# A two-layer decoder trunk in split float32: two loads of each weight tile in place of three

## The chip, the cores and the metric

The kernel runs on one core of a Trainium2 chip. The metric is device time in microseconds of one execution. Three runs of the kernel before gave 2343.18, 2343.87 and 2344.66 us; the median is 2343.87.

## The reference

Two layers run over 264 tokens, 256 of a prompt and 8 samples, which share the weights (the samples come with states of their own). Everything is float32. Per layer:

```
n = rmsnorm(x);  z = n @ W_in                      # 2048 x 5136, columns split among four groups
  A short gated conv   B GLA (gated linear attention)   C long causal conv   D spatial gating
x = x + concat(A, B, C, D) @ W_o                   # 2048 x 2048
x = x + (silu(m @ W_gate) * (m @ W_up)) @ W_down   # m = rmsnorm(x); 2048 x 5632, 5632 x 2048
```

A final rmsnorm follows, and the new states are returned as well.

## The kernel before

**Layout.** Activations lie feature-major: xs is [128 features, 16 tiles, 264 tokens]. A weight matrix is stationary, 128x128 at a time, and the 264 tokens are the moving columns, so that one matmul makes 128 output features of all tokens in PSUM.

**Split products.** TensorE runs on fp32r operands, which keep fewer bits than float32. So each operand is split into a high part (a rounded copy, made by ScalarE) and a low part (the rest, made by VectorE): weights into wh and wl (lines 285 and 286), activations into xh and xl, hh and hl, or the y tiles (split_x, emit_y, ev_ab, ev_u). A product is the sum of three: wh with the high activations (L300), wh with the low ones (L301), wl with the high ones (L302). For each of them the 128x128 weight tile is loaded anew, so wh is loaded twice and wl once.

**stream.** All large products go through stream (line 265): 512 output columns of a matrix, four column tiles m of 128, over all its row tiles of 128. It works in chunks of KC = 2 row tiles: SyncE's queue loads 512 KB into raw (four buffers), ScalarE makes wh, VectorE makes wl (three buffers each), and TensorE does for each of the four column tiles and two row tiles the three matmuls. Four PSUM banks collect the sums over the whole stream; then evac(m, psum) takes each away. There are 80 streams and 752 chunks: per layer ten of the projection W_in (c2, c1, r, q with k, v, vd, u, ac, ax, ab, in this order; r has 16 columns more, in a fifth bank, lines 304 to 314), four of W_o, 22 of gate and up (pairs, 512 columns each), four of W_down.

**PSUM.** Eight banks: five in the pool ps_w, three in ps_m. In the projections, in W_o and in the first pair of gate and up, a stream's sums come from ps_w alone (the small products of the layer use ps_m); with wide=True they go round all eight by the counter turn.

**Work beside the streams.** Per projection stream VectorE and ScalarE evacuate four tiles and do what the groups need. The long convolution (cc, line 474) runs in the background on VectorE: step_back puts 1.75 of its instructions on average behind each chunk's wl.

**The order.** The kernel is written through a tile framework. It has a scheduler which orders each engine's instructions when the program is built; each engine then runs its list in order and waits by semaphores for operands and for buffers to come free. What is written next to each other need not stand so in the list.

Of the kernel before, what the change touches and what calls it, by code (L numbers as in the profile page):

```python
# [17 lines left out]
P = 128  # L18
# [12 lines left out]
KC = 2  # L31
CW = 31
COL = dict(ax=0, ab=512, ac=1024, q=1536, k=1792, v=2048, r=2560, lr=3072,
# [7 lines left out]
def hybrid_trunk_kernel(  # L41
# [13 lines left out]
    raw_p = ctx.enter_context(tc.tile_pool(name="raw", bufs=4))  # L55
    sp_p = ctx.enter_context(tc.tile_pool(name="sp", bufs=3))
# [49 lines left out]
    xs = act.tile([P, KT, T], F32, tag="xs", name="xs")  # L106
    xh = act.tile([P, KT, T], F32R, tag="xh", name="xh")
    xl = act.tile([P, KT, T], F32R, tag="xl", name="xl")
    xhs = [xh[:, k, :] for k in range(KT)]
    xls = [xl[:, k, :] for k in range(KT)]  # L110
# [37 lines left out]
    # Sample tokens: the parts of both convolutions that lie in the states, in three pieces  # L148
# [30 lines left out]
    def newton(var, y, hv, t, inv=1.0):  # L179
        """y = 1/sqrt(inv * var + eps) to full float32 precision."""  # L180
# [16 lines left out]
    def token_means(ps, c0, src, ones, start=True, stop=True):  # L197
        """ps[:, c0:c0+3] = column means of src [P, T], for tokens 0.., 128.. and the last 128."""
# [4 lines left out]
    def split_x(par, row):  # L203
        """Split of gain * x for the tensor engine."""
        for k in range(KT):
            g = par[:, k % 4, row + k // 4:row + k // 4 + 1]
            actf(xh[:, k, :], xs[:, k, :], AF.Identity, scale=g)
            stt(out=xl[:, k, :], in0=xs[:, k, :], scalar=g, in1=xh[:, k, :].bitcast(F32),
                op0=ALU.mult, op1=ALU.subtract)

    def add_squares(acc, g):
        """acc += squares of x tiles 2g, 2g+1."""
# [18 lines left out]
    def rms_x(acc):  # L231
        """1/rms of x on every partition, from the sums of squares of its tiles."""
# [9 lines left out]
    def step_back(ins):  # L242
        """Some instructions of the work in the background, behind ins on VectorE."""
# [21 lines left out]
    def stream(W, col0, ncol, kts, rh, rl, evac, wide=False):  # L265
# [6 lines left out]
        for m in range(nm):  # L272
            turn[0] = (turn[0] + 1) % 8
            if wide and turn[0] >= 5:
                pts.append(psm("pwx"))
            elif m < 4:
                pts.append(ps_w.tile([P, T], F32, tag="w", name=f"pw{m}"))
            else:
                pts.append(psm("pwx"))
        for c in range(0, len(kts), KC):  # L280
            k0 = kts[c]
            r = early.pop(0) if early else load_w(W, len(kts) * P, col0, ncol, k0)
# [7 lines left out]
            if back:  # L290
                step_back(sub)
            for m in range(nm):
                for j in range(KC):
                    kk = k0 + j
                    first = c == 0 and j == 0
                    last = c + KC >= len(kts) and j == KC - 1
                    if m < 4:
                        o = pts[m][:, :T]
                        a = wh[:, j, m * P:(m + 1) * P]
                        mm(out=o, lhsT=a, rhs=rh[kk], start=first, stop=False)  # L300
                        mm(out=o, lhsT=a, rhs=rl[kk], start=False, stop=False)  # L301
                        mm(out=o, lhsT=wl[:, j, m * P:(m + 1) * P], rhs=rh[kk],  # L302
                           start=False, stop=last)
                    else:
                        def both():
                            mm(out=pts[m][:2 * nx, :T], lhsT=wh[:, j, 512:512 + 2 * nx],
# [713 lines left out]
```

## Time and profile before

| what | value |
|---|---|
| median of the runs | 2343.87 us |
| profiled execution: span | 2341.9 us |
| TensorE, mean granted clock | 0.993 |
| DMA, mean over the span | 176 GB/s, 412.44 MB |
| TensorE waiting for VectorE's wl | 14.4 us in 9 waits |

The page of the profile gives each engine's busy time, the chain of work that ended last, and the costliest groups of instructions (line, engine, operation, output and inputs, shapes, count, busy time, mean length, idle time before and what ended it). PE is TensorE, PEld its weight loads, which run beside it, DVE is VectorE, ACT ScalarE. A timeline gives start, length and row; windows give, for a stretch, busy time and count of each engine, the granted clock (PEclk) and the share of the DMA engines. The profiled execution took the span plus what lies around it; the median stands 2.0 us above the span.

### The profile page before, as it was taken

To read this page: it belongs to the slowest core of one execution; us is meant where nothing else is said; L and a number is where in the kernel's file an instruction comes from. 1 tells how busy PE (TensorE), PEld (TensorE's weight loads), DVE (VectorE), ACT (ScalarE), POOL (GpSimd) and SP (SyncE) were. 2 spreads that over 40 slices of the span, in tenths; PEclk is the share of its full clock that TensorE was granted. 3 is DMA by queue.
4 is the path that set the end of the run, shared out by engine and by line. 5 is a ranking of instruction groups with operands and counts; after the bars stand their busy time and mean duration, and the time that the engine had idled before them with its cause. 6 is when DMAs were issued, how large, how long until landed. Compare 5 with 4: busy or idle time off the path is not lost.

```text
span 2341.9 us, 44256 instructions
## 1 busy us (share of the span) xinstructions
PE 2300.4 (98%) x18656; PEld 2275.3 (97%) x18656; DVE 1464.6 (63%) x2084; ACT 1003.0 (43%) x1248; POOL 214.0 (9%) x266
## 2 busy tenths in 40 slices
PE   9989999999999999999998999999999999999997
PEld 8889999999999999999998999999999999999997
DVE  6999966555655555444469998665555555544444
ACT  5534454444444444444344445444444444433433
POOL 3852000000000000000039110000000000000000
PEclk9999999999999999999999999999999999999999
DMA  7436555555555555555563455555555555555553
GB/s 237 139 117 183 171 185 185 180 179 183 180 188 182 181 182 181 180 179 179 180 200 124 136 182 169 186 179 182 181 180 180 189 180 181 182 181 178 174 178 128
DMA packets 208875, 412.44 MB, mean 176 GB/s; under 512 B 14001, under 2 KB 14067, under 8 KB 208644
## 3 DMA queue, kind: packets, MB, share of 16 engines
q1 hardware_dynamic: 204644, 400.53, 52.5%
q0 software_dynamic: 4032, 9.09, 1.5%
q8 instruction: 146, 2.39, 0.4%
q14 instruction: 53, 0.43, 0.1%
HBM read 404.25 MB, written 6.29 MB: 175 GB/s over the span
## 4 chain that ended last, share of the span: by engine, by line
PE 92%; DVE 5%; issue 1%; DMA 1%; ACT 0%; POOL 0%; SPq 0%; DVEq 0%; ACTq 0%
PE pw L300 22%; PE pw L301 22%; PE pw L302 22%; PE pwx L300 8%; PE pwx L301 8%; PE pwx L302 8%; DVE wl L286 1%; DVE cc L474 1%; DVE qd L593 1%; DVE bb L538 0%; DVE att L603 0%; PE ps_os L710 0%; PE ps_lv L601 0%; DMA raw<-in_w_in_dram 0%; DVE dd L586 0%
## 5 line engine op out<-in xcount | busy, mean ns | idle before, releaser
L286 DVE TENSOR_TENSOR wl<-raw,wh 128x1024 fp32r<-128x1024 f32 x752 | 932.4, 1241 | 734.2 <-ACT wh L285 733.3
L285 ACT ACTIVATE wh<-raw 128x1024 fp32r<-128x1024 f32 (+1 forms) x752 | 795.8, 1060 | 1197.7 <-PE pw L301 680.9
L302 PE MATMUL pw<-xh,wl 128*128 128x264 f32 x3136 | 887.3, 287 | 14.5 <-DVE wl L286 14.4
L300 PE MATMUL pw<-xh,wh 128*128 128x264 f32 x3136 | 894.9, 287 | 6.3 <-DVE qk L548 2.9
L301 PE MATMUL pw<-xl,wh 128*128 128x264 f32 x3136 | 893.5, 286 | 0.0
L302 PEld LDWEIGHTS pw<-xh,wl 128*128 128x128 f32 x3136 | 590.1, 190 | 18.3 <-DVE wl L286 16.6
L300 PEld LDWEIGHTS pw<-xh,wh 128*128 128x128 f32 x3136 | 593.6, 190 | 10.5 <-DVE qk L548 3.3
L301 PEld LDWEIGHTS pw<-xl,wh 128*128 128x128 f32 x3136 | 593.8, 189 | 5.6 <-issue 5.0
L300 PE MATMUL pwx<-xh,wh 128*128 128x264 f32 x960 | 273.0, 285 | 0.0
L302 PE MATMUL pwx<-xh,wl 128*128 128x264 f32 x960 | 272.4, 284 | 0.0
L301 PE MATMUL pwx<-xl,wh 128*128 128x264 f32 x960 | 272.3, 284 | 0.0
L301 PE MATMUL pw<-hl,wh 128*128 128x264 f32 x880 | 250.8, 286 | 0.0
L300 PE MATMUL pw<-hh,wh 128*128 128x264 f32 x880 | 250.4, 285 | 0.0
L302 PE MATMUL pw<-hh,wl 128*128 128x264 f32 x880 | 248.9, 285 | 0.0
L300 PEld LDWEIGHTS pwx<-xh,wh 128*128 128x128 f32 x960 | 180.9, 189 | 0.1
L302 PEld LDWEIGHTS pwx<-xh,wl 128*128 128x128 f32 x960 | 180.9, 189 | 0.0
L301 PEld LDWEIGHTS pwx<-xl,wh 128*128 128x128 f32 x960 | 180.7, 188 | 0.0
L300 PEld LDWEIGHTS pw<-hh,wh 128*128 128x128 f32 x880 | 165.9, 189 | 0.0
L301 PEld LDWEIGHTS pw<-hl,wh 128*128 128x128 f32 x880 | 165.8, 188 | 0.0
L302 PEld LDWEIGHTS pw<-hh,wl 128*128 128x128 f32 x880 | 165.2, 189 | 0.1
L301 PE MATMUL pwx<-hl,wh 128*128 128x264 f32 x528 | 150.8, 286 | 0.0
L300 PE MATMUL pwx<-hh,wh 128*128 128x264 f32 x528 | 150.2, 285 | 0.0
(303 smaller groups left out, 2413.8 us busy)
## 6 DMA issues: line engine op xcount, KB each, us to landing
raw<-in_w_gate_dram SPq DMA_DIRECT2D x176, 512.0 KB
raw<-in_w_up_dram SPq DMA_DIRECT2D x176, 512.0 KB
raw<-in_w_down_dram SPq DMA_DIRECT2D x176, 512.0 KB
raw<-in_w_in_dram SPq DMA_DIRECT2D x144, 512.0 KB
raw<-in_w_o_dram SPq DMA_DIRECT2D x64, 512.0 KB
raw<-in_w_in_dram SPq DMA_DIRECT2D x16, 528.0 KB
xp<-in_x_prompt_dram SPq DMA_DIRECT2D x4, 512.0 KB
s<-in_state_gla_dram POOLq DMA_DIRECT2D x16, 128.0 KB, 7.5
```

What stands on the lines that cost most here:

```text
L285: actf(wh[:, :, :ncol], r[:, :, :ncol], AF.Copy)
L286: sub = tt(out=wl, in0=r[:, :, :512], in1=wh[:, :, :512].bitcast(F32), op=ALU.subtract)
L300: mm(out=o, lhsT=a, rhs=rh[kk], start=first, stop=False)
L301: mm(out=o, lhsT=a, rhs=rl[kk], start=False, stop=False)
L302: mm(out=o, lhsT=wl[:, j, m * P:(m + 1) * P], rhs=rh[kk], start=False, stop=last)
L474: yield stt(out=cc[:, t, 0:NPT], in0=cext[:, t, k:k + NPT], scalar=col(t, k), in1=cc[:, t, 0:NPT], op0=ALU.mult, op1=ALU.add)
L593: tt(out=qd[half(r), q, :, r, :].rearrange("p s (n w) -> p s n w", w=h), in0=qz[half(r), q, 0:NPT].rearrange("p (s n w) -> p s n w", s=2, ...
```

## The change

High and low activations of a tile now lie side by side in one tile of 528 columns (xw, hw, yw, yaw): 264 high, then 264 low. With LB = 136 the products of a row tile become:

- wh with the first 400 columns, that is all high and the first 136 low ones, in one matmul (L324), into a bank of 400 columns: sums of the high part in 0:264, of those low ones in 264:400;
- wl with the 264 high columns (L325), as before;
- the other 128 low columns become stationary themselves: 128 tokens by 512 output columns, one matmul with wh as the moving side for all four column tiles (L313), into a bank pp of its own.

At the end of a stream ScalarE copies pp to SBUF (psb), and four matmuls with psb as the stationary side and the identity as the moving one transpose it into the columns 136:264 of the four sums (last_low, L297). The 136 low columns in 264:400 are added by VectorE: in W_o and W_down straight into xs (add_x, two additions for a tile where there was one), elsewhere after a ScalarE copy (L343, L344) into the sums in PSUM, before evac. A stream thus takes five banks where it took four. The high and low parts of the y tiles are split per smaller tile and lie in other buffers of the mixer (s0, vb, t10, qk). The arithmetic is the same sum of three products.

The diff, cut to its core:

```
+LB = 136
+    xw = act.tile([P, KT, 2 * T], F32R, tag="xw", name="xw")
+    def split_plain(w, src):
+        h, lo = (w[:, :T], w[:, T:]) if len(w.shape) == 2 else (w[:, :, :T], w[:, :, T:])
+        actf(h, src, AF.Copy)
+        tt(out=lo, in0=src, in1=h.bitcast(F32), op=ALU.subtract)
+
+    def add_x(i, ps, low):
+        tt(out=xs[:, i, :], in0=xs[:, i, :], in1=ps, op=ALU.add)
+        tt(out=xs[:, i, :LB], in0=xs[:, i, :LB], in1=low, op=ALU.add)
...
-        for m in range(nm):
+        for m in range(-1, nm):
             turn[0] = (turn[0] + 1) % 8
-            if wide and turn[0] >= 5:
+            if m == 4 or wide and turn[0] >= 5:
                 pts.append(psm("pwx"))
...
+        pp, pts = pts[0], pts[1:]
+        def last_low(m):
+            mm(out=pts[m][:, LB:T], lhsT=psb[:, m * P:(m + 1) * P], rhs=ident_r, start=False, stop=True)
...
+            for j in range(KC):
+                mm(out=pp, lhsT=xws[k0 + j][:, T + LB:], rhs=wh[:, j, :512],
+                   start=c == 0 and j == 0, stop=end and j == KC - 1)
+            if end:
+                psb = lo_p.tile([P, 512], F32R, tag="psb", name="psb")
+                actf(psb, pp, AF.Copy)
...
-                        mm(out=o, lhsT=a, rhs=rh[kk], start=first, stop=False)
-                        mm(out=o, lhsT=a, rhs=rl[kk], start=False, stop=False)
-                        mm(out=o, lhsT=wl[:, j, m * P:(m + 1) * P], rhs=rh[kk],
-                           start=False, stop=last)
+                        mm(out=pts[m][:, :T + LB], lhsT=hi, rhs=x[:, :T + LB], start=first, stop=False)
+                        mm(out=pts[m][:, :T], lhsT=lo, rhs=x[:, :T], start=False, stop=False)
...
+                if end and 1 <= m < 4:
+                    last_low(m - 1)
+            if end:
+                last_low(3)
         for m in range(nm):
+            o = pts[m][:P if m < 4 else 2 * nx]
+            low = o[:, T:T + LB]
+            if parts:
+                evac(m, o[:, :T], low)
+                continue
+            t = tmp.tile([P, LB], F32, tag="t1", name="low", bufs=6)[:P if m < 4 else 2 * nx]
+            actf(t, low, AF.Copy)
+            tt(out=o[:, :LB], in0=o[:, :LB], in1=t, op=ALU.add)
+            evac(m, o[:, :T])
```

Three places of the order follow; a name's number tells one buffer from another.

TensorE, first layer, from the end of the stream vd (sums pw..., the last chunk's wh and wl) to the first chunks of the stream u (pw0). Before:

```order
L301 MATMUL pw3_2197<-xl_94,wh_2422 128x264
L302 MATMUL pw3_2197<-xh_93,wl_2423 128x264
L300 MATMUL pw0_2517<-xh_93,wh_2523 128x264
L301 MATMUL pw0_2517<-xl_94,wh_2523 128x264
L302 MATMUL pw0_2517<-xh_93,wl_2524 128x264
```

Now, at the same place (pw-1 is the bank pp of the new stream):

```order
L325 MATMUL pw3_2059<-xw_96,wl_2243 128x264
L297 MATMUL pw0_2056<-ident_r_97,psb_2250 128x128
L297 MATMUL pw1_2057<-ident_r_97,psb_2250 128x128
L297 MATMUL pw2_2058<-ident_r_97,psb_2250 128x128
L297 MATMUL pw3_2059<-ident_r_97,psb_2250 128x128
L313 MATMUL pw-1_2349<-wh_2356,xw_96 128x512 x2
L313 MATMUL pw-1_2349<-wh_2381,xw_96 128x512 x2
L313 MATMUL pw-1_2349<-wh_2407,xw_96 128x512 x2
L324 MATMUL pw0_2350<-xw_96,wh_2356 128x400
L325 MATMUL pw0_2350<-xw_96,wl_2357 128x264
```

The four small products stand at the end of the old stream, and the low-row products of three chunks stand ahead of the new stream's first column tile.

VectorE at the same edge; dv is the evacuation of vd, os and cc are other work, wl are the splits of the new stream's chunks. Before:

```order
L286 TENSOR_TENSOR wl_2555<-raw_2552,wh_2554 128x1024
L474 SCALAR_TENSOR_TENSOR cc_915<-cext_259,par0_827,cc_915 128x256
L751 TENSOR_TENSOR dv_2192<-pw0_2194,rb_634 128x264
L751 TENSOR_TENSOR dv_2192<-pw1_2195,rb_634 128x264
L474 SCALAR_TENSOR_TENSOR cc_915<-cext_259,par0_827,cc_915 128x256
L751 TENSOR_TENSOR dv_2192<-pw2_2196,rb_634 128x264
L718 COPY_PREDICATED os_2139<-smask_90,ps_os_2094 32x128
L751 TENSOR_TENSOR dv_2192<-pw3_2197,rb_634 128x264
L718 COPY_PREDICATED os_2139<-smask_90,ps_os_2094 32x128 x2
L286 TENSOR_TENSOR wl_2587<-raw_2584,wh_2586 128x1024
```

Now:

```order
L306 TENSOR_TENSOR wl_2408<-raw_2405,wh_2407 128x1024
L502 SCALAR_TENSOR_TENSOR cc_861<-cext_263,par0_773,cc_861 128x256
L199 TENSOR_TENSOR nt_2011<-hv_2009,rs_2010 128x9
L344 TENSOR_TENSOR pw0_2056<-pw0_2056,low_2272 128x136
L344 TENSOR_TENSOR pw1_2057<-pw1_2057,low_2277 128x136
L344 TENSOR_TENSOR pw2_2058<-pw2_2058,low_2282 128x136
L344 TENSOR_TENSOR pw3_2059<-pw3_2059,low_2287 128x136
L502 SCALAR_TENSOR_TENSOR cc_861<-cext_263,par0_773,cc_861 128x256
L200 TENSOR_TENSOR nt_2011<-nt_2011,rs_2010 128x9
L779 TENSOR_TENSOR dv_2053<-pw0_2056,rb_592 128x264
```

The split of the new stream's third chunk (wl_2408) stands ahead of the evacuation of the first tile, where the third one (wl_2587) stood behind all four; the four additions stand ahead of it too.

TensorE in the feed-forward stage of the first layer, between an up stream and the next gate stream (the old sums are 6912 to 6915, the new ones 7149 to 7152), now:

```order
L313 MATMUL pw-1_7148<-wh_7179,xw_96 128x512
L297 MATMUL pw0_6912<-ident_r_97,psb_7092 128x128
L297 MATMUL pw1_6913<-ident_r_97,psb_7092 128x128
L297 MATMUL pw2_6914<-ident_r_97,psb_7092 128x128
L297 MATMUL pw3_6915<-ident_r_97,psb_7092 128x128
L324 MATMUL pwx_7151<-xw_96,wh_7155 128x400
```

Here the small products stand inside the new stream; its fourth column tile (pw3_7152) comes first 25 matmuls after them.

More of the change, by code (lines that the diff above doesn't have):

```diff
@@ L106, in hybrid_trunk_kernel @@
     xs = act.tile([P, KT, T], F32, tag="xs", name="xs")
[L107 to L110, printed above, removed]
+    xw = act.tile([P, KT, 2 * T], F32R, tag="xw", name="xw")
+    xws = [xw[:, k, :] for k in range(KT)]
+    ident_r = cst.tile([P, P], F32R, tag="ident_r", name="ident_r")
+    nc.vector.tensor_copy(ident_r, ident)
+    def split_plain(w, src):
[5 more added lines that the diff above has]
+        tt(out=xs[:, i, :LB], in0=xs[:, i, :LB], in1=low, op=ALU.add)
     def load_rows(l, dma):
@@ L263, in load_w, with stream @@
         return r
-    def stream(W, col0, ncol, kts, rh, rl, evac, wide=False):
+    def stream(W, col0, ncol, kts, xws, evac, wide=False, parts=False):
         nm = (ncol + P - 1) // P
@@ L315, in stream @@
-        for m in range(nm):
-            evac(m, pts[m][:P if m < 4 else 2 * nx, :T])
+                        hi, lo = (w[:, j, m * P:(m + 1) * P] for w in (wh, wl))
+                        mm(out=pts[m][:, :T + LB], lhsT=hi, rhs=x[:, :T + LB], start=first, stop=False)
+                        mm(out=pts[m][:, :T], lhsT=lo, rhs=x[:, :T], start=False, stop=False)
+                    else:
+                        o = pts[m][:2 * nx]
+                        w = wh[:, j, 512:512 + 2 * nx]
+                        mm(out=o[:, :T + LB], lhsT=w, rhs=x[:, :T + LB], start=first, stop=False)
+                        mm(out=o[:, LB:T], lhsT=w, rhs=x[:, T + LB:], start=False,
+                           stop=end and j == KC - 1)
@@ L835, in mixer_phase, with ev_o @@
         for g in range(4):
-            def ev_o(m, ps, g=g):
-                i = 4 * g + m
-                tt(out=xs[:, i, :], in0=xs[:, i, :], in1=ps, op=ALU.add)
-            stream(w_o[l], g * 512, 512, order, yh, yl, ev_o)
+            def ev_o(m, ps, low, g=g):
+                add_x(4 * g + m, ps, low)
+            stream(w_o[l], g * 512, 512, order, yws, ev_o, parts=True)
         es.close()
@@ L904, in ffn_phase @@
         ff = es.enter_context(tc.tile_pool(name="ff", bufs=1, reuse_waits="tile"))
-        hh = ff.tile([P, FT, T], F32R, tag="hh", name="hh")
-        hl = ff.tile([P, FT, T], F32R, tag="hl", name="hl")
+        hw = ff.tile([P, FT, 2 * T], F32R, tag="hw", name="hw")
+        hws = [hw[:, i, :] for i in range(FT)]
         split_x(par, ROW["nf"])
@@ L937, in ev_u @@
                 tt(out=u, in0=u, in1=t, op=ALU.mult)
[L938 to L941 removed]
+                split_plain(hws[i], u)
+            stream(w_gate[l], g * 512, 512, list(range(KT)), xws, ev_g, wide=wide)
             if l + 1 < DEPTH and 2 <= g <= 5:
@@ L947, in ffn_phase, with ev_d @@
                     prep_state(npar, g - 3, past, *nxt[2])
-            stream(w_up[l], g * 512, 512, list(range(KT)), xhs, xls, ev_u, wide=wide)
+            stream(w_up[l], g * 512, 512, list(range(KT)), xws, ev_u, wide=wide)
         for g in range(4):
-            def ev_d(m, ps, g=g):
-                i = 4 * g + m
-                tt(out=xs[:, i, :], in0=xs[:, i, :], in1=ps, op=ALU.add)
+            def ev_d(m, ps, low, g=g):
+                add_x(4 * g + m, ps, low)
                 if l + 1 == DEPTH and g == 3:
                     fin_tile(g, m, par)
-            stream(w_down[l], g * 512, 512, list(range(FT)), [hh[:, i, :] for i in range(FT)],
-                   [hl[:, i, :] for i in range(FT)], ev_d, wide=True)
+            stream(w_down[l], g * 512, 512, list(range(FT)), hws, ev_d, wide=True, parts=True)
             if l + 1 == DEPTH:
```

67 lines of the change are left out of this document (24 added, 43 removed).

## Prediction

> **What bounds the kernel now.** I read the page first: the busy shares, then the chain that ended last, then the costliest groups.
>
> ```profile
> span 2341.9 us, 44256 instructions
> PE 2300.4 (98%) x18656; PEld 2275.3 (97%) x18656; DVE 1464.6 (63%) x2084; ACT 1003.0 (43%) x1248; POOL 214.0 (9%) x266
> PE 92%; DVE 5%; issue 1%; DMA 1%; ACT 0%; POOL 0%; SPq 0%; DVEq 0%; ACTq 0%
> L286 DVE TENSOR_TENSOR wl<-raw,wh 128x1024 fp32r<-128x1024 f32 x752 | 932.4, 1241 | 734.2 <-ACT wh L285 733.3
> L285 ACT ACTIVATE wh<-raw 128x1024 fp32r<-128x1024 f32 (+1 forms) x752 | 795.8, 1060 | 1197.7 <-PE pw L301 680.9
> ```
>
> TensorE carries 92% of the chain. Each of the 752 chunks is split once by ScalarE (1.06 us) and once by VectorE (1.24 us), and both then wait for TensorE. A chunk holds two row tiles of 128 rows, so there are 1504 row tiles with four column tiles each, and three matmuls for each of those: 18048 of the 18656 matmuls are the ones that the change rewrites. Next I asked what one of them costs in time, from stretches where TensorE never stops.
>
> ```profile
> core 0: us, PE busy (x) PEld busy (x) DVE busy (x) ACT busy (x) POOL busy (x), PEclk, DMA share, GB/s
> 200.00:250.00 50.00, 50.00 (x394) 47.89 (x393) 46.40 (x97) 23.24 (x32) 1.25 (x2) 1.00 0.57 173
> 250.00:300.00 50.00, 50.00 (x413) 49.61 (x412) 45.09 (x81) 23.29 (x29) 2.20 (x5) 1.00 0.53 170
> 600.00:700.00 100.00, 100.00 (x826) 99.83 (x826) 55.52 (x73) 41.28 (x50) 0.00 (x0) 1.00 0.56 184
> 900.00:1000.00 100.00, 100.00 (x822) 100.00 (x821) 50.34 (x57) 40.39 (x45) 0.00 (x0) 1.00 0.55 179
> ```
>
> 826 and 822 matmuls in 100 us are 121.1 and 121.7 ns each; I take 121.4. (A matmul's recorded length, some 285 ns, is not its cost: the next one starts before it ends.) The question of the whole change is what these 121.4 ns are made of: columns, or something paid once per matmul or per load. Two places of the trace speak to it. After VectorE had let TensorE wait 7.74 us in the second layer, the granted clock was half for a while:
>
> ```profile
> 1271.58 0.59 PE L302 MATMUL pw<-xh,wl 128*128 128x264 f32 x1 [7.74 <-DVE wl L286]
> 1271.97 0.42 PE L300 MATMUL pw<-xh,wh 128*128 128x264 f32 x1
> ...
> 1276.37 0.42 PE L302 MATMUL pw<-xh,wl 128*128 128x264 f32 x1
> 1272.00:1276.00 4.00, 4.00 (x20) 4.00 (x20) 4.00 (x5) 1.93 (x5) 4.00 (x5) 0.50 0.44 131
> ```
>
> From the second row to the third, 20 matmuls start in 4.40 us, 220 ns each, at clock 0.50. If that is pure columns, 264 columns take 110.0 ns at full clock, and 11.4 ns of the 121.4 are something else. The second place has short loads:
>
> ```profile
> 77.53 0.40 PE L311 MATMUL pwx<-xl,wh 128*16 128x264 f32 x2
> 77.76 0.41 PE L306 MATMUL pwx<-xh,wh 128*32 128x264 f32 x2
> ...
> 78.72 0.28 PE L306 MATMUL pwx<-xh,wh 128*32 128x264 f32 x1
> L300 PEld LDWEIGHTS pw<-xh,wh 128*128 128x128 f32 x3136 | 593.6, 190 | 10.5 <-DVE qk L548 3.3 <-DVE vz L643 2.6 <-issue 1.7
> L311 PEld LDWEIGHTS pwx<-xl,wh 128*16 128x16 f32 x32 | 3.0, 95 | 0.6
> ```
>
> From 77.53 to 78.72 ten matmuls start (the merged rows hold two each), 119 ns each, though their loads have 16 or 32 columns and last 95 ns where 128 columns last 190. The load's length is thus hidden already; what a dropped load can save is at most the fixed 11.4 ns.
>
> **The change part by part.** *Fewer, longer matmuls.* A row tile had 12 matmuls of 264 columns, 3168 in all. It now has 4 of 400, 4 of 264 and 1 of 512: again 3168 columns, in 9 matmuls. If the 11.4 ns are paid per matmul, each row tile saves 3 x 11.4 = 34.2 ns, and 1504 of them 51.4 us. If they grow with the columns, it saves nothing. No row has another width at this type, so both ends stay; I take 51.4, since the half-clock rows show nothing beside columns once the array is slow, which looks like a start-up gap that a slower stream hides.
>
> A rule speaks against the change: the Trainium skill, "TensorE: Matmul & The Clock Gate", section "Wait — 56ns, not 53.3ns?", gives N / 1.2 GHz while cold and N / 2.4 GHz plus some 2.5 ns when warm. The trace agrees cold (220 ns) and not warm (121.4 against 112.5). By the Trainium skill's 2.5 ns the saving would be 3 x 2.5 x 1504 = 11.3 us. The Trainium skill, same page, section "What happens when you issue a matmul", says that loads are pulled ahead of running matmuls, so that the next weights load while this tile runs; the 95 and 190 ns loads with one spacing agree.
>
> *The 128-column products.* Each of the 80 streams now ends with four transposing matmuls, 128 columns with 128 stationary ones, 320 in all. The nearest rows are transposes of that size in another type:
>
> ```profile
> 220.07 0.27 PE L733 MATMUL ps_oT<-ident,ot 128*128 128x128 f32 x1
> 221.23 0.49 PE L733 MATMUL ps_oT<-ident,ot 128*128 128x128 f32 x3
> ```
>
> Three take 0.49 us where one takes 0.27, so they start 0.11 us apart. Below, 128 columns and the fixed part give 53 + 11 = 65 ns; above, a full 121. I take 0.11, the row itself: 320 x 0.11 = 35.2 us (20.8 to 38.7), all on TensorE. Two thirds of the saving are gone again.
>
> *Evacuations.* ScalarE gains 80 copies psb of 128x512 from PSUM and 258 copies of 136 columns, VectorE about 322 additions of 136 columns. The nearest rows:
>
> ```profile
> L652 ACT ACTIVATE vT<-ps_vT 128x512 f32<-128x512 f32 x4 | 2.2, 596 | 4.3 <-PE ps_vT L651 4.3
> L432 ACT ACTIVATE sgm<-pw 128x264 f32<-128x264 f32 x4 | 1.5, 382 | 0.6 <-PE pw L302 0.6
> L161 DVE TENSOR_TENSOR pw<-ps_pc,par 128x480 f32<-128x480 f32 x4 | 2.5, 651 | 0.0
> L751 DVE TENSOR_TENSOR dv<-pw,rb 128x264 f32<-128x264 f32 x8 | 3.3, 429 | 0.7 <-PE pw L302 0.7
> ```
>
> By the slope between the two sizes of each engine, 136 columns are about 0.27 us on ScalarE and 0.30 on VectorE (estimates). In the feed-forward stage this is covered: VectorE is busy 50 to 56 of 100 us there, eight PSUM banks rotate over streams of five, and three of them are free when a stream begins. The first bank that the next stream must wait for is its fourth column tile's; in the new order 25 matmuls stand between the four small products and that tile, some 4 us, and the evacuation of the first tile takes about 2. I cost those edges at nothing; without that cover each would cost what follows.
>
> *The edges of the ten projections.* Here (and in the output projection and the first feed-forward group) a stream takes five banks and there are five. The new stream's bank for the low rows is free early, but its first column tile needs the bank of the old first column tile, where before a fifth bank was free. I worked one edge out, vd to u in the first layer, by the two orders shown above and these rows:
>
> ```profile
> 207.22 0.48 DVE L474 SCALAR_TENSOR_TENSOR cc<-cext,par,cc 128x256 f32<-128x256 f32 x1
> ```
>
> When the old stream's last matmul releases the split buffers, ScalarE makes the third chunk's high part (1.06), VectorE its low part (1.24), then cc (0.48), a small one, four additions (1.20), cc again (0.48), a small one and only then dv from the first bank (0.43): 0.1 each for the two small ones and for the hand-overs, about 5.2 us. TensorE has meanwhile four small products (0.44) and six 512-column matmuls (213 + 11 ns each, 1.35): it waits 3.4 us. Queued behind it in order stand all matmuls of the next stream, and behind those VectorE's further splits, which need their buffers. Before, the same stretch (200 to 250 us) has TensorE busy 50.00 of 50. The other edges have the same shape with 2.3 to 4.2 us; about 20 of them make some 60 us. Part comes back: VectorE is busy 46.40 and 45.09 of 50 us in those stretches and already holds TensorE up elsewhere, and a wait lets it catch up. The 56 additions of a layer alone are 17 us on it, where these two stretches leave it 8.5 of 100 us. I take 45 us. Below, nothing, if the waits only replace older ones; above, 75, if all count and the longer ones halve the clock as at 1272 us.
>
> *The end and the start.* Behind the last matmul stand one small product and one more addition: 1.5 us. The other edits (one buffer for both parts, the y tiles split elsewhere) make instructions of the same sizes in the same number: nothing.
>
> Sum: 2341.9 - 51.4 + 35.2 + 45 + 1.5 = 2372.2 us of span. The median of the runs shown, 2343.87, stands 2.0 above the profiled span, so 2374.
>
> **The rivals.** *The 11.4 ns go with the columns* (a stream that cannot be fed faster, say). For it: the short loads changed nothing, so the matmul itself is slow. Against: 220 ns fit the bare columns so well. Then nothing is saved: 2374 + 51.4 = 2426. By the Trainium skill's 2.5 ns (the page and section above) it would be 2374 + 51.4 - 11.3 = 2414.
>
> *The waits at the edges replace older ones*, and the kernel gets faster. Place: the bank of the first column tile at the 20 edges. VectorE, not TensorE, sets the pace in part of the projection stages:
>
> ```profile
> PE pw L302 <- DVE wl L286: 14.4, 9, 7.7
> ```
>
> If the time lost at an edge is made up at such places, only some 8 us remain: 2374 - 37 = 2337. It decides at (51.4 - 35.2 - 1.5) / 20 = 0.7 us per edge: under that the kernel is faster. Against it: those 14.4 us are nine waits in all, 7.7 of them in one.
>
> *The 11.4 ns are steps of 32 columns*: 264 would cost 288 (120.0) and 1.4. Then 400 cost 174.7 and 512 cost 214.7 ns, a row tile 1399 instead of 1457, and 86.8 us are saved: 2374 - 35.4 = 2339. Against it: nothing shows a step at half clock, where 264 columns cost 220.0, not 240.
>
> That the change does not do what it says is excluded by the order: nine matmuls stand where twelve stood.
>
> **How the numbers follow.** Forecast (fixed part per matmul, waits of 15 us and more) 0.50; columns 0.20; replaced waits 0.17; steps 0.10; something slower that I do not see 0.03. The forecast's own range, from the waits' bounds, is 2344 to 2404. What a measurement of this kernel can tell from no change is about 0.2%, 4.7 us. Faster: replaced waits and half of the steps, 0.22. Same: a share of the steps and the forecast's lower end, 0.08. Slower: 0.70. The range 2328 to 2426 leaves out the replaced waits at their best and the columns with all waits, about a tenth on each side.
>
> **What would show it.** In the feed-forward stage, a stream of 16 row tiles has 148 matmuls, and 100 us should hold about 638 of them if a row tile takes 1423 ns, 623 if 1457. The 512-column matmuls should start 0.225 us apart, 0.235 by columns; the small products 0.11. The waits should appear as TensorE waiting for VectorE's evacuations (vz, dv, uu, acz, uext, ya) with 2 to 4 us each, ten a layer. I am wrong if these waits are under 0.7 us, or if the feed-forward stage gets shorter by more than 2% (the sum says 0.5).

## The result and the profile after

The changed kernel takes 2484.32 us (median; 2483.07 to 2484.51), the kernel before 2343.86 on the same chip: ratio 1.0597, 95% interval 1.0582 to 1.0612. I had forecast 2374 and at most 2426. It is slower, as forecast, but by 140 us where I had 30. From the page of the changed kernel:

```profile
span 2482.5 us, 36757 instructions
...
PE 2345.1 (94%) x14464; PEld 2241.5 (90%) x14464; DVE 1514.9 (61%) x2415; ACT 1102.1 (44%) x1594; POOL 191.7 (8%) x266
```

The instructions are 7500 fewer, and TensorE's share fell from 98 to 94%: time is lost to waiting. Where, the stretches say, here of the changed kernel; columns: PE, PEld, DVE, ACT, POOL busy, granted clock, DMA share, GB/s:

```profile
100.00:200.00 100.00, 65.78 (x400) 61.29 (x399) 64.98 (x121) 35.86 (x61) 43.21 (x49) 0.83 0.30 91
...
250.00:300.00 50.00, 47.61 (x293) 45.39 (x292) 42.77 (x84) 23.06 (x36) 1.20 (x3) 0.95 0.45 141
600.00:700.00 100.00, 100.00 (x630) 97.06 (x629) 59.52 (x88) 47.48 (x71) 0.00 (x0) 1.00 0.56 179
```

and the first of them in the kernel before:

```profile
100.00:200.00 100.00, 91.43 (x684) 85.51 (x685) 95.16 (x161) 43.04 (x68) 57.38 (x58) 0.97 0.47 144
```

In the feed-forward stage TensorE is still never idle. In the first of these stretches every engine is *less* busy than before, VectorE too (65.0 of 100 us where it was 95.2). Nobody is overloaded there; the engines wait for each other. For whom, the waits of TensorE in the changed kernel say (us in total, times, longest):

```profile
PE pw L324 <- DVE rg L544: 57.0, 2, 28.5
PE ps_x L654 <- DVE eb L650: 10.9, 2, 5.5
PE pw L324 <- DVE qk L576: 8.5, 2, 4.3
PE pw L324 <- DVE acz L827: 5.7, 2, 3.1
...
PE pw L324 <- DVE dv L779: 5.4, 2, 2.7
...
PE pw L324 <- DVE xs L124: 2.1, 1, 2.1
```

The small ones are of the kind and near the size that I had forecast: some 1 to 5.5 us each, most of them behind VectorE's evacuations (the wait for eb is not behind one). The first is not: 28.5 us, once in each layer, at the start of the q stream. Its timelines (TensorE, VectorE, ScalarE and GpSimd of the changed kernel; start, duration):

```profile
135.29 0.67 PE L324 MATMUL pw<-xw,wh 128*128 128x400 f32 x1 [28.52 <-DVE rg L544]
...
134.37 0.31 DVE L344 TENSOR_TENSOR pw<-pw,low 128x136 f32<-128x136 f32 x1 [24.06 <-ACT low L343]
134.71 0.43 DVE L544 TENSOR_TENSOR rg<-pw,rb 128x264 f32<-128x264 f32 x1
...
134.05 0.28 ACT L343 ACTIVATE low<-pw 128x136 f32<-128x136 f32 x1 [28.07 <-POOL cc L533]
...
133.31 0.71 POOL L533 TENSOR_TENSOR cc<-cc,cz 128x256 f32<-128x256 f32 x1
...
134.89 3.95 POOL L533 TENSOR_TENSOR cc<-cc,cz 128x256 f32<-128x256 f32 x5
```

Read it backwards from the releasers in brackets. TensorE waits for rg, the evacuation of a bank. VectorE stands at the addition of low and waits for ScalarE. ScalarE stands at the copy low and waits 28 us for GpSimd's cc, which has nothing to do with low. But `low` is a tile of tag t1, a ring of six buffers, and cz, the products of the convolution on GpSimd, are tiles of the same ring, thirty of them ahead of it in the program. ScalarE must not write before GpSimd has read the cz that held the buffer; it is let go when the addition at 133.31 ends, with five more to come (the last row). Behind the waiting copy, in order, stand the next splits; so TensorE can't go on either.

The rest of the loss was found by comparing, stream by stream, when ScalarE begins a stream's first split. Such rows of the first layer stand below, in the kernel before (L285) and the changed one (L305), each the start of a stream: feed-forward streams 18 and 20, and the second and fourth down stream. Two feed-forward streams take 46.62 us before and 47.27 after, two down streams 129.03 and 128.89:

```profile
814.86 1.06 ACT L285 ACTIVATE wh<-raw 128x1024 fp32r<-128x1024 f32 x1 [1.84 <-PE pw L301]
...
861.48 1.06 ACT L285 ACTIVATE wh<-raw 128x1024 fp32r<-128x1024 f32 x1 [1.84 <-PE pw L301]
...
972.62 1.06 ACT L285 ACTIVATE wh<-raw 128x1024 fp32r<-128x1024 f32 x1 [1.88 <-PE pwx L301]
...
1101.65 1.06 ACT L285 ACTIVATE wh<-raw 128x1024 fp32r<-128x1024 f32 x1 [1.88 <-PE pwx L301]
```
```profile
882.44 1.06 ACT L305 ACTIVATE wh<-raw 128x1024 fp32r<-128x1024 f32 x1 [1.38 <-PE pw L324]
...
929.71 1.06 ACT L305 ACTIVATE wh<-raw 128x1024 fp32r<-128x1024 f32 x1 [1.38 <-PE pw L324]
...
1041.29 1.06 ACT L305 ACTIVATE wh<-raw 128x1024 fp32r<-128x1024 f32 x1 [1.83 <-PE pw L324]
...
1170.18 1.06 ACT L305 ACTIVATE wh<-raw 128x1024 fp32r<-128x1024 f32 x1 [1.83 <-PE pw L324]
```

A stream of 16 row tiles became 0.325 us longer, one of 44 row tiles 0.070 us shorter. If a row tile saves the same in both stages, that gives both prices: (0.325 + 0.070) / 28 = 14.1 ns saved for each row tile, and 0.325 + 16 x 0.0141 = 0.55 us paid for each stream's end. For 1504 row tiles and 80 streams: 21 us saved, 44 paid. Over the whole kernel, by the same start times: the twenty projections 113 us longer (the q and v streams 46 of them, vd 22), the eight output projections and the first two feed-forward streams of each layer 7.5, the other forty feed-forward streams 14, the down streams and the end 7; together 141.

### The profile page after: what moved, and what is told of

Same layout as the page of the kernel before. It is cut to its first block, busy times and chain, and to the rows that moved or that the text cites. A ratio compares the mean times of both kernels' runs of the same rounds, so it can differ in the third digit from the quotient of the medians.

```text
span 2482.5 us, 36757 instructions
## 1 busy us (share of the span) xinstructions
PE 2345.1 (94%) x14464; PEld 2241.5 (90%) x14464; DVE 1514.9 (61%) x2415; ACT 1102.1 (44%) x1594; POOL 191.7 (8%) x266
## 5 line engine op out<-in xcount | busy, mean ns | idle before, releaser
L305 ACT ACTIVATE wh<-raw 128x1024 fp32r<-128x1024 f32 (+1 forms) x752 | 789.2, 1059 | 1008.7 <-PE pw L324 684.1
L324 PE MATMUL pw<-xw,wh 128*128 128x400 f32 x3120 | 981.5, 353 | 89.4 <-DVE rg L544 57.0
L325 PE MATMUL pw<-xw,wl 128*128 128x264 f32 x3120 | 857.2, 289 | 3.0 <-DVE wl L306 3.0
L324 PEld LDWEIGHTS pw<-xw,wh 128*128 128x128 f32 x3120 | 595.3, 192 | 117.0 <-ACT low L343 57.8
L325 PEld LDWEIGHTS pw<-xw,wl 128*128 128x128 f32 x3120 | 599.5, 193 | 19.7 <-DVE wl L306 4.1
L324 PE MATMUL pwx<-xw,wh 128*128 128x400 f32 x976 | 305.4, 346 | 0.0
L324 PE MATMUL pw<-hw,wh 128*128 128x400 f32 x924 | 287.2, 345 | 2.1 <-DVE xs L124 2.1
L325 PE MATMUL pwx<-xw,wl 128*128 128x264 f32 x976 | 266.1, 284 | 0.0
L325 PE MATMUL pw<-hw,wl 128*128 128x264 f32 x924 | 257.1, 284 | 0.0
L325 PEld LDWEIGHTS pwx<-xw,wl 128*128 128x128 f32 x976 | 183.2, 188 | 4.2
L324 PEld LDWEIGHTS pwx<-xw,wh 128*128 128x128 f32 x976 | 182.2, 188 | 5.3
L324 PEld LDWEIGHTS pw<-hw,wh 128*128 128x128 f32 x924 | 173.0, 188 | 6.5 <-issue 2.5
L325 PEld LDWEIGHTS pw<-hw,wl 128*128 128x128 f32 x924 | 173.4, 188 | 3.6
L324 PE MATMUL pwx<-hw,wh 128*128 128x400 f32 x484 | 152.3, 345 | 0.9 <-ACT yo L903 0.9
L325 PE MATMUL pwx<-hw,wl 128*128 128x264 f32 x484 | 135.1, 284 | 0.0
L324 PE MATMUL pw<-yw,wh 128*128 128x400 f32 x384 | 114.1, 346 | 3.6 <-DVE ya L852 3.3
L325 PE MATMUL pw<-yw,wl 128*128 128x264 f32 x384 | 99.8, 283 | 0.0
L324 PEld LDWEIGHTS pwx<-hw,wh 128*128 128x128 f32 x484 | 90.6, 188 | 5.1 <-ACT yo L903 1.4
L325 PEld LDWEIGHTS pwx<-hw,wl 128*128 128x128 f32 x484 | 90.8, 188 | 3.4
L343 ACT ACTIVATE low<-pw 128x136 f32<-128x136 f32 x195 | 45.0, 278 | 94.9 <-POOL cc L533 56.1
```

The lines of the kernel that those rows point to most:

```text
L305: actf(wh[:, :, :ncol], r[:, :, :ncol], AF.Copy)
L324: mm(out=pts[m][:, :T + LB], lhsT=hi, rhs=x[:, :T + LB], start=first, stop=False)
L325: mm(out=pts[m][:, :T], lhsT=lo, rhs=x[:, :T], start=False, stop=False)
L343: actf(t, low, AF.Copy)
```

## The experiments

Times are medians, or single runs where that is said, beside runs of the kernel before on the same chip (2344 to 2345 us). Four runs of one kernel lie at most some 6 us apart.

**Buffers of its own for low.** Against the changed kernel:

```
-    lo_p = ctx.enter_context(tc.tile_pool(name="lo", bufs=2))
+    lo_p = ctx.enter_context(tc.tile_pool(name="lo", bufs=1))
...
-            t = tmp.tile([P, LB], F32, tag="t1", name="low", bufs=6)[...]
+            t = tmp.tile([P, LB], F32, tag="low", name="low", bufs=4)[...]
```

> The copies named low get buffers of their own (four, and psb one instead of two so that they fit) instead of sharing the ring of six t1 buffers with the convolution's products cz. Ring theory: the two waits of 28.9 us at the start of the q stream (TensorE waits for the bank, VectorE for low, ScalarE for a t1 buffer that GpSimd's cz still holds) shrink to an ordinary edge of about 4 us; of that some 4 us per layer is given back in the v stream, which was shorter after the long wait. 2484 - 2 x (28.9 - 4) + 2 x 4 = 2442, anywhere from 2428 to 2448. Bank and VectorE-load theory: the wait is made by the five banks and by VectorE's queue whatever the buffer of low is, and the time stays within 10 us of 2484.

Measured 2441.21 us (ratio to before 1.0411, 1.0395 to 1.0426), as the ring theory said. The ring is shown: 43 us of the 140 were a shared tag. The same wait of TensorE in this run:

```profile
PE pw L324 <- DVE rg L544: 8.6, 2, 5.6
```

**A bank from the other pool for the low rows of every narrow stream.** On top of the first run:

```
-            if m == 4 or wide and turn[0] >= 5:
+            if m < 0 and not wide or m == 4 or wide and turn[0] >= 5:
```

> As the run with buffers of their own for low, and besides the bank of the low rows (pp) of the narrow streams comes from the other pool of three, so that the column tiles rotate over five banks as they did before. Bank theory (my forecast's): the waits of 2 to 5 us of TensorE for dv, uu, acz, uext, ya, gs, qk at the starts of streams go, some 20 edges x 2.5 us = 50 us below the first run, about 2390. VectorE-load theory: the waits move to the splits or to the small products behind VectorE's queue, and the time stays within 12 us of the first run.

Measured 2500.85 us (ratio 1.0667, 1.0649 to 1.0685): neither. The wait for dv halves (5.4 us in the first run), but others grow; the waits of this run:

```profile
PE pw L325 <- DVE wl L306: 24.3, 23, 2.9
PE ps_dT L794 <- ACT dv L789: 14.1, 2, 7.1
...
PE pw L324 <- DVE dv L779: 2.7, 2, 1.4
```

Against the first run the streams v and u, in which TensorE makes many small products, became 15 to 19 us longer each; vd, which was 11 us longer already, 1 to 2. TensorE's small products need the pool of three, from which a bank was now taken for whole streams. That this is the reason is not shown: the rows name VectorE's splits (wl) and ScalarE (dv). As a test of the bank theory it is inconclusive, so it was repeated where few small products run.

**The spare bank only there.** On top of the first run, with `spare=True` for c1, ac, ax, ab, the output projection and the first up stream:

```
-            if m == 4 or wide and turn[0] >= 5:
+            if m < 0 and spare or m == 4 or wide and turn[0] >= 5:
```

> As the run with buffers of their own for low (2441), but in the streams during which TensorE makes few small products (c1, ac, ax, ab, the four of the output projection and the first up stream) the bank of the low rows comes from the pool of three, so that a column tile's bank is spare again. Bank theory: the waits for gs, cext, acz, uext, ya and the like at the starts of these streams go: nine streams a layer, 31 us in the two layers less 6 for what each stream costs anyway, about 2416. VectorE-load theory: TensorE starts the stream and then waits for the splits instead, over 2433.

Measured 2445.91 us (ratio 1.0435, 1.0419 to 1.0450), 5 us above the first run. The wait for acz falls from 4.5 to 1.3 us in the two layers, and others stand in its place (xs had 2.1 us in the first run, dv at L794 none):

```profile
PE pw L324 <- DVE xs L124: 8.1, 9, 2.1
...
PE ps_dT L794 <- ACT dv L789: 4.8, 2, 2.4
...
PE pw L324 <- DVE acz L827: 1.3, 2, 0.7
```

So my forecast's reason for the edges (the first column tile lacks its fifth bank) falls as the thing to mend: with the bank TensorE can start, and it then waits elsewhere for as long.

**Without the copy and the addition in the projections**, and **without the addition alone**. On top of the first run:

```
-            actf(t, low, AF.Copy)
-            tt(out=o[:, :LB], in0=o[:, :LB], in1=t, op=ALU.add)
+            if wide:
+                actf(t, low, AF.Copy)
+                tt(out=o[:, :LB], in0=o[:, :LB], in1=t, op=ALU.add)
```

> As the first run, and the projections, the output projection excepted, leave out the copy low and its addition (so the low parts of the first 136 columns are not added there; the feed-forward stage keeps them, its first group apart). Bank theory: the first column tile is evacuated 1.2 to 2 us earlier at each of 20 edges, 24 to 40 us below the first run, but a bank is still lacking and waits of 1 to 2 us stay at most edges. VectorE-load theory: what the change costs in the projections nearly vanishes, the wait of 5.5 us for eb too; 50 to 60 us below the first run, about 2385.

Measured 2374.14 us (one run), 67 below the first run and more than either theory gave. Then with the copy outside the condition:

> As the run without copy and addition in the projections (2374), but with ScalarE's copies of the low parts kept; only VectorE's additions are left out (the low parts of the first 136 columns are not added there). If VectorE's additions, 0.31 us each and in its queue ahead of the evacuations, are what costs 67 us: 2372 to 2384. If ScalarE's copies, behind which the evacuation stands only through the addition, take a good part: over 2395 is impossible by this theory unless the copies hold back the next splits; then 2390 to 2430.

Measured 2410.43 us (one run). Of the 67 us, 31 go with VectorE's additions and 36 with ScalarE's copies, though a copy is 0.28 us and no evacuation reads its result any more. One reading is that the copy holds the bank, which is free only when the copy too has been made. The trace of this run says otherwise; the edge from v to vd in the first layer, ScalarE, VectorE and TensorE:

```profile
173.69 0.79 ACT L343 ACTIVATE low<-pw 128x136 f32<-128x136 f32 x4
...
177.61 1.22 DVE L306 TENSOR_TENSOR wl<-raw,wh 128x1024 fp32r<-128x1024 f32 x1
178.74 1.45 DVE L672 TENSOR_TENSOR vz<-pw,rb 128x264 f32<-128x264 f32 x4
...
179.23 0.70 PE L324 MATMUL pw<-xw,wh 128*128 128x400 f32 x1 [3.44 <-DVE vz L672]
```

The four copies have ended at 174.5 us. TensorE waits for VectorE's evacuation vz, and that stands behind the split of the new stream's third chunk. At the starts of q, v and u of this layer, too, the last copy had ended 1.3 to 4.4 us before the end of the evacuation that let TensorE go. From q to ab in both layers, the evacuation stands behind three splits of the new stream at 12 of 14 edges with the copies, behind two at all 14 without them, and in the kernel before behind one at ten and two at four. So at these edges the copies cost through the order of VectorE's list: the bank is evacuated one split later. Why the order changes with the copies, no run shows. The next run takes VectorE out of what a bank waits for.

**One copy that frees the bank.** Against the changed kernel (psb and weight buffers 1 and 3 instead of 2 and 4, for room):

```
+            t = tmp.tile([P, T + LB], F32, tag="low", name="low", bufs=4)[...]
+            if wide:
+                t = t[:, T:]
+                actf(t, low, AF.Copy)
+            else:
+                actf(t, o[:, :T + LB], AF.Copy)
+                o, t = t, t[:, T:]
             tt(out=o[:, :LB], in0=o[:, :LB], in1=t, op=ALU.add)
```

> The changed kernel, but in the projections and the first feed-forward group ScalarE copies all 400 columns of a bank at once into a buffer of its own (0.48 us where the 136 columns took 0.28), and VectorE adds and scales from that buffer; three weight buffers instead of four make the room. A bank is then free as soon as ScalarE has copied it, and nothing on VectorE stands between. Theory of the release chain (last matmul, ScalarE's copy, VectorE's additions, evacuation, only then the bank): both the ring of t1 and the chain are out of the way, and with VectorE's work unchanged the time falls to 2375 to 2400. Theory of VectorE's load (it has as many instructions as before): not under 2430, since its splits come no earlier.

Measured 2389.56 us (ratio 1.0191, 1.0175 to 1.0206): 95 of the 140 us are gone: the ring's 43, and another 52 below the first run. Two of the stretches that had suffered, in this run:

```profile
100.00:200.00 100.00, 88.11 (x528) 80.25 (x527) 96.70 (x157) 48.47 (x76) 58.03 (x49) 0.95 0.43 127
...
250.00:300.00 50.00, 50.00 (x322) 48.11 (x321) 44.31 (x88) 26.04 (x39) 1.21 (x3) 1.00 0.53 162
```

TensorE is busy 88.1 and 50.0 us of them, where the first run has 79.0 and 47.6 and the changed kernel 65.8 and 47.6. VectorE is busy 96.7 of the first 100 us, where the first run has 85.3 and the changed kernel 65: it does *more* in the same time once TensorE does not wait for it. Over the whole kernel it has as many instructions as in the changed one (2415) and no less to do (1523.9 us against 1514.9), and its evacuations still stand behind three splits of the new stream. That is the release chain, not the load.

**The re-cut alone.** On top of the run without copy and addition:

```
-                if end and 1 <= m < 4:
-                    last_low(m - 1)
-            if end:
-                last_low(3)
...
-            if end:
-                psb = lo_p.tile([P, 512], F32R, tag="psb", name="psb")
-                actf(psb, pp, AF.Copy)
```

> As the run without copy and addition in the projections (2374), and besides without the copy psb and the four transposing products at the end of each of the 80 streams (the product of the high weights with the low parts of the last 128 columns is made but not added). What is left is the re-cut alone: 9 matmuls in place of 12. If a stream's end costs 0.56 us as the stage table says, 45 us less: 2329. If it costs the 0.44 us of my sum, 35 us less: 2339. As to the re-cut itself: by my forecast's 11.4 ns for each matmul dropped the result would be near 2344 - 51 = 2293, by 4.9 ns (14.6 ns a row tile) near 2322, by columns alone not under 2344; waits that are left come on top.

Measured 2324.43 us (one run), 50 below: 0.62 us for each end, the price of 0.55 and a few waits. With everything else stripped, nine matmuls in place of twelve are worth 20 us, far from the 51 of my sum. The streams of this run show both prices directly, by the same start times. A feed-forward stream takes 23.14 us (23.31 in the kernel before, 23.62 with the ends), a down stream 63.86 (64.51 and 64.41). So a row tile saves 10.4 ns in the one stage and 14.9 in the other, some 17 us in all where the 14.1 ns of above give 21; and an end costs 0.48 and 0.55 us, 39 in all where 0.55 throughout gives 44.

**The matmul's rate with nothing beside it.** Against the changed kernel:

```
-            r = early.pop(0) if early else load_w(...)
+            if not wide or c == 0:
+                r = early.pop(0) if early else load_w(...)
...
```

> The changed kernel, but from the second feed-forward group on, and in the down projections, only the first chunk of each stream is loaded and split, and its tiles are used for all chunks (so its output is not the reference's). TensorE's instructions are the same, and the transfers, ScalarE's copies and VectorE's subtractions are gone from that stage. If the matmuls run below 2.4 columns per ns because transfers and the other engines disturb them, a 264-column matmul falls from 121 towards 112 ns and the whole gets some 70 to 100 us shorter (2390 to 2410). If the rate is the matmul's own in this type, 264, 400 and 512 columns stay at 121, 183 and 232 ns and the time stays within 8 us of 2484.

Measured 2472.47 us (one run). The feed-forward stage in it, with an eighth of the transfers (22 GB/s) and less than half of VectorE's and ScalarE's work:

```profile
800.00:900.00 100.00, 100.00 (x629) 97.08 (x628) 23.54 (x56) 17.37 (x41) 0.00 (x0) 1.00 0.07 22
```

629 matmuls in 100 us, and 630 with everything running. The rate is the matmul's own; transfers and the other engines do not disturb it. The time misses the 8 us around 2484 by 4, but not because of the rate. By the start of each stream's first product, 6.5 of the 12 us lie in the projections, which this edit leaves alone, 4.3 in the last layer's down streams and the end behind them, and 1.5 in the forty feed-forward streams.

**The long convolution on other engines.** Since GpSimd was what the long wait ended on, its share was varied. Two of four channel tiles on GpSimd, in the kernel before (`range(2)` on VectorE, `range(2, 4)` on GpSimd, 1.2 steps a chunk):

> The kernel before, with two of the long convolution's four channel tiles on GpSimd instead of one, and VectorE's share at 1.2 instead of 1.75 steps a chunk. If VectorE is what holds TensorE up in the projections of the kernel before too, its waits there (14.4 us for the splits, and the half clock after them) shrink: 2325 to 2340. If those waits come from the chain of small steps for the gates, nothing changes (2341 to 2346); GpSimd's other work standing behind the second tile could make it slower.

Measured 2368.44 us (ratio 1.0101, 1.0084 to 1.0118), slower; what made it so was not isolated. Then none on GpSimd, in both kernels:

```
-            for t in range(3):
+            for t in range(4):
...
-        for t in range(3, 4):
-            c = cc[:, t, 0:NPT]
...
-        back.append((conv_all(), fin_c, 1.75))
+        back.append((conv_all(), fin_c, 2.33))
```

> The changed kernel with all four channel tiles of the long convolution on VectorE (2.33 steps a chunk instead of 1.75), so that no cz is made and GpSimd is idle there; low stays in the ring of t1. Ring theory: the two waits of 28.9 us go although low has no buffers of its own. VectorE has 32 more steps of 0.48 us a layer, but its subtraction of 128x1024, which took 1.55 to 1.79 us while GpSimd worked and takes 1.22 otherwise, is faster: 2430 to 2450, about as the run with buffers of its own (2441). If the wait had come from something else on VectorE's queue, it stays: 2480 and more.

> The kernel before with the same edit: the whole long convolution on VectorE. Two channel tiles on GpSimd had made it 24 us slower. If that is because GpSimd slows VectorE down (the subtraction of 128x1024 takes 1.65 us beside it and 1.22 alone), then none on GpSimd is faster than one: 2325 to 2340, faster than both kernels. If VectorE's 32 more steps a layer (15 us) weigh more, where it is busy 95 of 100 us: 2348 to 2365.

Measured: the changed kernel 2438.75 us (one run), with low still in the ring of t1; no cz, no wait, the ring shown a second time. The kernel before 2321.23 us (ratio 0.9902, 0.9885 to 0.9918), **faster than both kernels** and 4 us below the range expected. What goes with it, in the busiest groups of VectorE from 70 to 135 us, before and with the whole convolution on VectorE:

```profile
L286 DVE TENSOR_TENSOR wl<-raw,wh 128x1024 fp32r<-128x1024 f32 x15 | 24.8, 1651 | 2.0 <-ACT wh L285 2.0
L474 DVE SCALAR_TENSOR_TENSOR cc<-cext,par,cc 128x256 f32<-128x256 f32 x29 | 21.3, 735 | 0.3
```
```profile
L286 DVE TENSOR_TENSOR wl<-raw,wh 128x1024 fp32r<-128x1024 f32 x17 | 20.8, 1221 | 4.1 <-ACT wh L285 3.9
L474 DVE SCALAR_TENSOR_TENSOR cc<-cext,par,cc 128x256 f32<-128x256 f32 x40 | 19.9, 498 | 0.6
```

VectorE made 40 steps and 17 splits in less time than 29 and 15 beside GpSimd. The Trainium skill ("SBUF — State Buffer", section "Who interferes with whom") states that a VectorE instruction with two inputs in SBUF contends with a GpSimd instruction that reads SBUF, and that the order of issue decides which of them blocks. Both of these instructions have two such inputs, and the rows agree (1651 against 1221 ns).

**Both repairs together**, in the changed kernel, and the same with the convolution's steps at 2.7 a chunk, beside the kernel before with 2.7:

> Both repairs of the changed kernel together: one copy of 400 columns to free a bank, and the whole long convolution on VectorE. If what is left of the change is its own price (ends of streams 45 us, re-cut minus 22 us, the last evacuations some 9 us), it stands 32 us above the kernel before with the same convolution (2321): 2353, up to 2368 with waits that stay. If the two repairs remove the same waits, it stays at the first's 2385 to 2390. Faster than 2344 would mean that the prices of the ends were wrong.

> The changed kernel with both repairs, and VectorE's background steps of the convolution at 2.7 instead of 2.33 a chunk, so that it ends some 7 chunks (20 us) earlier. In the run before (2381) TensorE waited 8.7 and 8.5 us for yw at the start of the output projection, and the clock was half behind that: if this is a side effect of the repair, it goes, and 2355 to 2364 is reached, what the change's own price says. If the rest belongs to the change, the time stays within 6 us of 2381.

> The kernel before with the whole convolution on VectorE (2321), at 2.7 steps a chunk. TensorE waits some 2.7 us at the start of the output projection there in each layer: 2314 to 2320 if these go, up to 2330 if the denser steps hold up the splits in the projections instead. The difference between the two runs of this call is the change's own price: 35 to 45 us expected.

Measured 2381.04 (ratio 1.0157, 1.0140 to 1.0174), 2385.97 (1.0177, 1.0160 to 1.0194) and 2324.36 us (0.9913, 0.9898 to 0.9928). Neither number expected for the first was met, and the denser steps did not mend it. The two kernels with the same convolution stay 60 and 62 us apart, where 32 and 35 to 45 were expected; by the start times of the first pair, 24 of the 60 lie in the output projections and the first feed-forward streams, 15 in the projections, 12 in the other feed-forward streams and 9 in the down streams and the end. Where the first of these come from, the waits tell: TensorE still waits for yw in the first stream of the output projection, 9.2 us in the second of these runs. The last step of the convolution and the end of its normalisation on VectorE in the first layer, at 2.33 steps a chunk, and at 2.7, and the wait behind it in the list of TensorE's waits:

```profile
274.54 0.48 DVE L507 SCALAR_TENSOR_TENSOR cc<-cext,par,cc 128x256 f32<-128x256 f32 x1
...
317.71 1.26 DVE L452 TENSOR_TENSOR cc<-cc,rsl 128x1056 f32<-128x1056 f32 x1
```
```profile
257.12 0.47 DVE L507 SCALAR_TENSOR_TENSOR cc<-cext,par,cc 128x256 f32<-128x256 f32 x1
...
316.14 1.26 DVE L452 TENSOR_TENSOR cc<-cc,rsl 128x1056 f32<-128x1056 f32 x1
```
```profile
PE pw-1_3329 L313 <- DVE yw L120: 10.6, 2, 9.2
```

The convolution ended 17 us earlier, and its normalisation, spread over VectorE's queue, at the same time. The kernel before with the convolution on VectorE does likewise: its last step starts at 264.6 us, or 251.1 with the denser steps, and the normalisation ends at 299.4 and 301.0. That more steps a chunk do not bring it forward is thus no trait of the change. But there TensorE waits for the high and low parts of y (yh, yl) only 2.5 us in the two layers. Why the normalisation stands so late in the changed kernel's order that TensorE waits for it, stays open. The change was not brought below the kernel before, and the fastest version is the kernel before with its convolution on VectorE, 2321 us.

## Why the prediction was wrong, point by point

**The fixed part per matmul: the term was mis-sized.** I read 11.4 ns beside the columns and charged them to each matmul, 51.4 us. Matmuls of three widths, of the changed kernel in the feed-forward stage:

```profile
1904.37 0.63 PE L313 MATMUL pwx<-wh,xw 128*128 128x512 f32 x2
1904.84 0.29 PE L325 MATMUL pwx<-xw,wl 128*128 128x264 f32 x1
1904.96 0.35 PE L324 MATMUL pwx<-xw,wh 128*128 128x400 f32 x1
1905.15 0.28 PE L325 MATMUL pwx<-xw,wl 128*128 128x264 f32 x1
```

From start to start 264 columns take 0.12 us, 400 take 0.19 (the medians over all are 121 and 183 ns) and 512 take 0.235 (232). By the 220 ns of 264 columns at half clock, 110, 167 and 213 ns were to be expected; the rest is 11, 16 and 19 ns, so the excess grows with the columns. The row tile saves 10 to 15 ns, not 34.2, which leaves 3.5 to 5 ns paid for each matmul. The feed-forward stage holds 630 matmuls in 100 us, half-way between the 638 and 623 that I had set. The rival of the columns was the nearer one. The step that failed is the inference from the half clock: 220 ns for 264 columns did not show that what is beside the columns at full clock is paid once. By the Trainium skill ("TensorE: Matmul & The Clock Gate", section "Wait — 56ns, not 53.3ns?") 2.5 ns per matmul would have been saved, 11 us; the measured 3.5 to 5 lie nearer to that than to my 11.4, though the spacing of 121 ns is not the one that the section gives.

**The 128-column products: right in kind, 4 to 9 us short.** The end of a stream in the same kernel:

```profile
1916.68 0.22 PE L297 MATMUL pwx<-ident_r,psb 128*128 128x128 f32 x1
1916.74 0.49 PE L297 MATMUL pw<-ident_r,psb 128*128 128x128 f32 x3
1917.08 0.39 PE L324 MATMUL pwx<-xw,wh 128*128 128x400 f32 x1
```

Four take 0.40 us (0.06, then 0.11 each), near my 0.44; the stream's end costs 0.48 to 0.55 by the stage times. What makes up the rest I have not isolated.

**The edges: the shape right, the sum of their causes not.** 45 us were taken and 110 measured; this is the step that failed by most. One part is the 43 us of the ring, which my sum has at nothing. I followed a bank from ScalarE's copy to VectorE's evacuation and asked of every operation which engine it stands behind, but not which *buffer* it writes and who read that buffer last; the line that creates `low` names the tag t1, and the convolution's line names it too. My 0.27 us for the copy was right and beside the point. The other part is the 67 us of copies and additions. Their place and their sizes (1 to 8 us in the first run, behind rg, qk, eb, dv, acz and others) were near the forecast, and so was the sum of the waits; the pages of the first run and of the run without copy and addition:

```profile
PE 2347.1 (96%) x14464; PEld 2242.7 (92%) x14464; DVE 1514.7 (62%) x2415; ACT 1093.0 (45%) x1594; POOL 209.5 (9%) x266
...
PE 2324.7 (98%) x14464; PEld 2224.3 (94%) x14464; DVE 1490.0 (63%) x2317; ACT 1073.0 (45%) x1496; POOL 216.2 (9%) x266
```

Of spans of 2440.0 and 2372.1 us, TensorE is idle 92.9 and 47.4 us: 45 of the 67 are waits, as much as I had taken for all edges together. The other 22 are the same 14464 matmuls taking longer, at a mean granted clock of 0.983 against 0.994: a wait slows what follows. The window behind the long wait of the changed kernel shows that most plainly:

```profile
135.00:142.00 7.00, 6.71 (x31) 6.39 (x31) 2.67 (x10) 3.34 (x9) 3.53 (x5) 0.72 0.01 2
```

The granted clock averages 0.72 over 7 us, and TensorE starts 31 matmuls in them where the feed-forward stage has 44. That I had named as the upper bound's case (75 us) and left out of the forecast.

**That part of the waits only replaces older ones: near.** TensorE's waits for VectorE's splits, 14.4 us in the kernel before, are 3.0 in the changed kernel and 5.1 in the first run. So 9 to 11 us of older waits went where I had taken 15 off; that this is VectorE catching up is not shown. The rival by which nearly all of the new waits replace older ones is out: TensorE is idle 51 us more in the first run than in the kernel before (92.9 against 41.5).

**The feed-forward edges at nothing: nearly right.** Forty streams became 14 us longer together, which 0.55 us an end and 14.1 ns a row tile explain. The edge into the last layer's second down stream is an exception (3.1 us longer): TensorE waits 2.1 us there for the second of the two additions to xs that now stand on VectorE for each tile (L124, in the list above).

**The end: 1.5 us forecast**, 4 measured (the last down stream's 90.2 us against 86.3), with four more additions to xs on VectorE behind the last product.

The balance, by the prices of the stage times: 30 us less saved, 9 more for the ends, 65 more for the edges (43 of the ring, 22 of the slower clock) and 6 for the end and that exception make the 110 us between 2374 and 2484. (By the prices of the re-cut alone it is 34 and 4 in place of 30 and 9.)

## What to carry to other kernels

Before adding a small tile to a kernel, look up every other user of its tag, and ask which instruction, on which engine, reads the buffer last: a ring joins engines that share no data. Cost an evacuation by the whole chain until the bank is free, with the place at which it stands in its engine's list, and shorten that chain before looking for more banks. Count behind a wait not only the idle time but also the slower clock. A gap between the measured spacing of one matmul width and an ideal rate says nothing about whether it is paid per matmul; two widths do.

## What the runs showed of the hardware

- In this type the spacing of a matmul at full clock is about 0.45 ns a column (121 ns for 264, 183 for 400, 232 for 512 columns), and 100 us hold as many matmuls (629 and 630) with 22 GB/s of transfers and VectorE at 24 us as with 179 GB/s and 60 us; at half clock 264 columns took 220 ns, without such an excess. What the excess is, no run here tells.
- VectorE's subtraction of 128x1024 took 1651 ns on average while GpSimd worked beside it and 1221 ns without, and its step of the convolution 735 and 498 ns. Giving half of the convolution to GpSimd made the kernel 24 us slower, giving it none made it 23 us faster.
- The same 14464 matmuls kept TensorE busy 2347.1 us at a mean granted clock of 0.983 and 2324.7 us at 0.994: beside 45 us more of waiting, 22 us more of slower matmuls.
